# Second layer of a four-layer decoder: gate projections as 16 more columns of the first head's v, and v ahead of q and k

## The chip, the cores and the metric

The kernel runs on one NeuronCore of one Trainium2 chip. The metric is the device time of one execution in microseconds (us). TensorE (PE) multiplies matrices and loads its weights beside that (PEld), VectorE (DVE) and ScalarE (ACT) work on rows of up to 128 partitions, GpSimd (POOL) does small copies and memsets, SyncE (SP) issues the DMAs. Each engine takes its own instructions strictly in the order in which they stand.

## The reference

1040 tokens (16 of a learnt prefix and 1024 of input) of 1024 features pass four layers; each adds a branch to the residual: `h = h + branch(rmsnorm(h, norm_gain[i]))`. Layers 1 and 4 are sliding-window attention, layer 3 is a gated recurrence (HGRN2), and layer 2, which the change touches, is an mLSTM with 8 heads. What matters of it:

```
q, k, v, ig, fg, og, z = split(u @ w_in, (1024, 1024, 2048, 8, 8, 2048, 2048))
q, k = split(silu(causal_conv(concat(q, k), conv_w, conv_b)))     # 4 taps
log_i = ig + bias_i                                               # 8 rows, one for each head
log_f = log_sigmoid(fg + bias_f)
h = chunkwise over blocks of 128 tokens, from q, k, v, log_i, log_f, state C and norm n
h = rmsnorm(sigmoid(og) * h, h_gain) * silu(z);   out = h @ w_out
```

The two gates are thus 16 columns of the big projection, and every head needs them, with running sums and maxima over the tokens, before its first block.

## The kernel before

The activations stand transposed: 8 tiles of 128 features by 1040 tokens, in the residual `x` and, after the norm, split in a high and a low part (`uh`, `ul`), so that a product in full precision is three matmuls (high by high, high by low, low by high) on the fp32r path. Weights come by DMA into `wr` (two buffers) and are split the same way by ACT (`wh`) and DVE (`wl`) into three pairs of buffers; the helper `split` does this everywhere (L187 ACT, L188 DVE). Tokens are worked in three chunks of 400, 384 and 256 (`CHUNKS`), or in 9 blocks (16 tokens, then 8 of 128), of which the chunks hold four, three and two. `proj` (L254) multiplies weights as the stationary side by a chunk of tokens; `proj_v` (L295, L299) takes tokens as the stationary side and 256 columns of v as the moving side, one block at a time, in two halves of the features.

The order of PE is written by hand: every layer hands over a list of steps (cost, function, and a step that fetches its weights ahead), `weave` mixes two lists by their costs, and steps of cost 0 stand for work without matmuls. A layer's `head` runs between the output projection of the layer before and its own `body`; the norm of the second and third chunk (`Norm`: squares, one statistic matmul at L381, eight units at L407 that end in `uh` and `ul`) is placed inside of it. The other engines' order is made by a scheduler from that program, and depends on it.

In the second layer (`layer_b`) the head is, for each chunk, the gates' projection (`gate_rows_proj`, L215: 16 matmuls with one tile that holds the gates' high and low weights), then q and k of head 0. Its result is put together by `gate_evac` (ACT L791, DVE L792). After the last chunk `gate_rows` computes, on 8 partitions by 1040 tokens, log-sigmoid (ACT L797 to L799, DVE L800), a running maximum (L801), running sums by block (L804), their differences (L806, L807) and an exponential (ACT L811). Two results go through DRAM (`rowsd`, L814 and L815) and come back broadcast to 128 partitions (`rb`, `wb`: L882, L883); the other two are transposed on PE by `gate_cols` (L825, L826). `conv_proj` takes q and k out of PSUM (ACT L846), applies the four taps on DVE (L849 and three times L852), and multiplies by the sigmoid (ACT L424 to L426, DVE L427, ACT L428, then DVE L856 for q and L858 for k). The body is v of head 0 with `gate_cols` in its middle, then the `mixer` of each head, woven with the next head's q, k and v. The first step of a mixer's block, `s1`, multiplies k by q and transposes k (L890, L892); its next step, `s2` (L918), needs the decayed weights that DVE and ACT make from `rb` (L903 and on).

Of the kernel before, what the change touches and what calls it, by code (L numbers as in the profile page):

```python
# [36 lines left out]
TAIL_LAG = 2000.0  # L37
PRIO = 40
ROWS, TMPS, RAWS, YS, QS = 9, 5, 2, 3, 6
XS = 14  # L40
GAP, BURST, PAUSE = 200.0, 1300.0, 2500.0
KT_LAG = 500.0
NORM_AT = (4000.0, 0.7), (5000.0, 0.5), (8000.0, 0.5)
# [6 lines left out]
MM = 1.0 / 2.4  # L50
# [18 lines left out]
def flat(groups):  # L69
    return [x for grp in groups for x in grp]  # L70
# [38 lines left out]
def hybrid_kernel(ctx: ExitStack, tc: tile.TileContext, ins, out, layers=(0, 1, 2, 3)):  # L109
    nc = tc.nc  # L110
    v, s, g, pe, sp = nc.vector, nc.scalar, nc.gpsimd, nc.tensor, nc.sync
# [11 lines left out]
    def nm(x):  # L123
        ctr[0] += 1
        return f"{x}{ctr[0]}"
# [11 lines left out]
        return tpool.tile([P, 404], F32, tag="t", name=nm("t"), bufs=TMPS)  # L137

    def small(w):
        return tpool.tile([P, w], F32, tag=f"s{w}", name=nm("s"), bufs=12 if w < 8 else 4)  # L140

    def psum(tag, bufs):
        return ps.tile([P, 512], F32, tag="p", name=nm(tag), bufs=8)
# [1 line left out]
    def psj():  # L145
        return psum("pj", 3)
# [6 lines left out]
    ident = cpool.tile([P, P], F32, name="ident")  # L153
# [32 lines left out]
    def split(src, h, l):  # L186
        s.copy(h, src)  # L187
        v.tensor_tensor(l, src, h.bitcast(F32), op=ALU.subtract)  # L188

    def gate_weights(src):  # L190

        w = wpool.tile([P, 1024], F32R, tag="wh", name=nm("wh"), bufs=3).rearrange("p (k z c) -> p k z c", k=KT, z=2)
        raw = wpool.tile([P, 512], F32, tag="raw", name=nm("wr"), bufs=RAWS)
        sp.dma_start(raw, src)
        raw = raw.rearrange("p (k c) -> p k c", k=KT)
        split(raw, w[:, :, 0], w[:, :, 1])
        return w

    def gate_rows_proj(src, evac):

        st = {}

        def pre():
            st["w"] = gate_weights(src)

        groups = []
        for n, (c0, cn) in enumerate(CHUNKS):
            grp = []
            for part in range(4):
                def fn(n=n, c0=c0, cn=cn, part=part):  # L210
                    if part == 0:
                        st[n] = psj()
                    for k in (2 * part, 2 * part + 1):
                        for i, b in enumerate((uh, ul)):
                            pe.matmul(st[n][:, :cn], st["w"][:, k].rearrange("p z c -> p (z c)"), b[:, k, c0 : c0 + cn],  # L215
                                      start=(k == 0 and i == 0), stop=(k == KT - 1 and i == 1))
                    if part == 3:
                        evac(st[n], n, c0, cn)

                grp.append([4 * cn * MM, fn, pre if (n == 0 and part == 0) else None])  # L220
            groups.append(grp)
        return groups

    def weights(src, kind, inrow=False):
        if inrow:
            h, l = (rrow()[:, :1024] for _ in range(2))
        else:
            h = wpool.tile([P, 1024], F32R, tag="wh", name=nm("wh"), bufs=3)
            l = wpool.tile([P, 1024], F32R, tag="wl", name=nm("wl"), bufs=3)
        for z in (slice(0, 512), slice(512, 1024)):  # L230
            raw = wpool.tile([P, 512], F32, tag="raw", name=nm("wr"), bufs=RAWS)
            sp.dma_start(raw, src[:, z])
            split(raw, h[:, z], l[:, z])
        k = dict(m=8, v=4, o=2)[kind]
        return h.rearrange("p (k c) -> p k c", k=k), l.rearrange("p (k c) -> p k c", k=k)
# [24 lines left out]
            groups.append(grp)  # L260
        return groups

    def put_v(V, acc, b, cn):

        if b == 0:
            s.copy(V[:cn, :256], acc[32 : 32 + cn, :256])
            v.tensor_tensor(V[:cn, :256], V[:cn, :256], acc[:cn, :256], op=ALU.add)
        else:
            s.copy(V[:cn, :256], acc[:cn, :256])

    def proj_v(src0, src1, evac):
        st = {}

        def pre0():
            st[0] = weights(src0, "v")

        def pre1():
            st[1] = weights(src1, "v")

        groups = []  # L280
        for blocks in CHUNK_BLOCKS:
            grp = []
            for b in blocks:
                c0, cn = blk(b)
                for half in range(2):
                    def fn(b=b, c0=c0, cn=cn, half=half):
                        if half == 0:
                            st["a", b] = psj()
                        acc = st["a", b]
                        wh, wl = st[half]  # L290
                        for kk in range(4):
                            k = 4 * half + kk
                            if b == 0:
                                for m in (wh, wl):
                                    pe.matmul(acc[:48, :256], um[:, k, :], m[:, kk, :],  # L295
                                              start=(k == 0 and m is wh), stop=(k == KT - 1 and m is wl))
                            else:
                                for i, (a, m) in enumerate(((uh, wh), (uh, wl), (ul, wh))):
                                    pe.matmul(acc[:cn, :256], a[:, k, c0 : c0 + cn], m[:, kk, :],  # L299
                                              start=(k == 0 and i == 0), stop=(k == KT - 1 and i == 2))  # L300
                        if half == 1:
                            evac(acc, b, c0, cn)

                    grp.append([(8 if b == 0 else 12) * 256 * MM, fn, (pre0, pre1)[half] if b == 0 else None])
            groups.append(grp)
        return groups

# [463 lines left out]
    def layer_b(i, j, fin):  # L771
        win, wout = ins["b_win"][j], ins["b_wout"][j]
        R = {}
# [10 lines left out]
            R["hgain"] = cols[:, 80:96]  # L784
            R["li"], R["lf"] = row(), row()

        def gate_evac(acc, n, c0, cn):
            cs = slice(c0, c0 + cn)
            for key, r, c in (("li", 0, 0), ("lf", 32, 1)):
                z = R[key][:8, cs]  # L790
                s.activation(z, acc[64 + r : 72 + r, :cn], AF.Identity, bias=R["bias"][:, c : c + 1])  # L791
                v.tensor_tensor(z, z, acc[r : r + 8, :cn], op=ALU.add)  # L792

        def gate_rows():
            mix, li, lf = R["mix"], R["li"], R["lf"]
# [66 lines left out]
        def v_evac(h):  # L862
            def f(acc, b, c0, cn):
                hi_ = rpool.tile([P, 258], F32R, tag="v", name=nm("v"), bufs=10)
                lo = R["mix"].tile([P, 256], F32R, tag="vl", name=nm("vl"), bufs=10)
                R["v", h, b] = hi_, lo
                if b == 0:
                    both = tmp()
                    put_v(both, acc, b, cn)
                    acc = both  # L870
                split(acc[:cn, :256], hi_[:cn, :256], lo[:cn])
# [140 lines left out]
        gg = gate_rows_proj(ins["b_wgate"][j], gate_evac)  # L1012
        qg = {h: conv_proj(win[8 * h], h, 1.0, ("q", h)) for h in range(8)}
        kg = {h: conv_proj(win[8 * h + 1], 8 + h, 128 ** -0.5, ("k", h)) for h in range(8)}
        vg = {h: proj_v(win[8 * h + 2], win[8 * h + 3], v_evac(h)) for h in range(8)}
        og = {h: og_proj(h) for h in range(8)}
        zg = {h: [gate_proj(win[8 * h + 6 + c], lambda h=h, c=c: R["h", h, c]) for c in range(2)] for h in range(8)}
        oc = {h: proj_out(wout[2 * h], wout[2 * h + 1], lambda k, h=h: R["h", h, k], CHUNKS,
# [7 lines left out]
                tail = g1[n] + tail  # L1026
            return flat(g0) + tail

        head = [gg[n] + qg[0][n] + kg[0][n] for n in range(3)]
        head[0].insert(0, [0.0, enter, None])  # L1030
        head[2].insert(len(gg[2]), [0.0, gate_rows, None])
        body = flat(vg[0])
        body.insert(len(body) // 2, [18 * 30, gate_cols, None])
        for h in range(8):
            mx = mixer(h)
            mx, rest = mx[:-3], mx[-3:]
# [9 lines left out]
        body = [z for z in body if z[1] is not pause]  # L1046
# [332 lines left out]
    k = 0  # L1379
# [31 lines left out]
def _layout(inp):  # L1411
# [50 lines left out]
    gw = np.zeros((D, 64), np.float32)  # L1462
    gw[:, 0:8] = bw[:, i0 : i0 + 8]
    gw[:, 32:40] = bw[:, f0 : f0 + 8]
    f["b_wgate"] = gw.reshape(KT, P, 64).transpose(1, 0, 2).reshape(1, P, 512)
# [40 lines left out]
```

## Time and profile before

| | us |
|---|---|
| runs | 2610.01, 2610.45, 2611.44 (median 2610.45) |
| profiled execution | 2610.83 |
| its span | 2609.0 |
| PE busy, of the span | 2558.0 |
| DVE busy | 1980.3 |
| ACT busy | 1725.9 |
| second layer's head and first body | about 488 to 553 of the span |

The span is the profiler's, from the first to the last instruction; 1.8 us of the execution's own time lie around it. Busy time of PE counts overlapping matmuls as one stretch, so it says when PE had work, and not how fast it went.

### The profile page before, as it was taken

How to read it: one execution, taken by the hardware profiler on the slowest of the kernel's cores; microseconds unless marked ns; L12 is line 12 of the kernel's file. 1: busy time of each engine (PE TensorE's matmuls, PEld its weight loads, DVE VectorE, ACT ScalarE, POOL GpSimd, SP SyncE). 2: the span in 40 equal slices, each digit the busy share in tenths (PEclk: the TensorE clock that was granted, in tenths of full speed). 3: DMA queues.
4: the chain of work that ended last, by engine and by line, in shares of the span. 5: the costliest groups of instructions: out<-in, count | busy, mean ns of one | idle time of the engine just before them, and what ended most of it. 6: DMA issues, size and time to landing. Idle time of an engine off the chain costs nothing.

```text
span 2609.0 us, 56062 instructions
## 1 busy us (share of the span) xinstructions
PE 2558.0 (98%) x21048; PEld 2459.0 (94%) x21048; DVE 1980.3 (76%) x5487; ACT 1725.9 (66%) x4757; POOL 154.1 (6%) x538
## 2 busy tenths in 40 slices
PE   7999999999999999999999999999999999999999
PEld 6899889899999999999999999999999999999999
DVE  6677777986767676767677788978787978677776
ACT  6777776566464646464646857878585867768872
POOL 1100100000000000000000000201001011000000
PEclk9999999999999999999999999999999999999999
DMA  4111111021111111111110101011110111111112
GB/s 136 56 43 50 46 37 47 17 67 58 41 58 41 58 41 58 41 58 41 55 61 34 57 27 42 30 38 34 34 42 26 42 62 45 54 44 47 53 38 82
DMA packets 74048, 126.81 MB, mean 49 GB/s; under 512 B 11552, under 2 KB 25760, under 8 KB 73776
## 3 DMA queue, kind: packets, MB, share of 16 engines
q1 hardware_dynamic: 73776, 123.23, 14.5%
q8 instruction: 165, 2.70, 0.4%
q14 instruction: 107, 0.88, 0.1%
HBM read 108.34 MB, written 4.26 MB: 43 GB/s over the span
## 4 chain that ended last, share of the span: by engine, by line
PE 81%; DVE 10%; ACT 6%; issue 1%; DMA 1%; POOL 0%; SPq 0%; DVEq 0%; ACTq 0%; POOLq 0%
PE pj L254 39%; PE pj L337 16%; PE pj L299 11%; PE po L682 2%; PE pt L660 1%; PE pm L614 1%; PE pm L615 1%; DVE t L407 1%; PE pa L534 1%; DVE ul L188 1%; PE po L918 1%; PE pj L295 1%; PE pm L890 1%; DVE X L1153 1%; DVE X L1155 1%
## 5 line engine op out<-in xcount | busy, mean ns | idle before, releaser
L254 PE MATMUL pj<-uh,wh 128*128 128x384 f32 (+2 forms) x2592 | 870.9, 336 | 3.7 <-ACT uh L187 3.6
L254 PE MATMUL pj<-ul,wh 128*128 128x384 f32 (+2 forms) x2592 | 835.3, 322 | 2.9 <-DVE ul L188 2.8
L254 PE MATMUL pj<-uh,wl 128*128 128x384 f32 (+2 forms) x2592 | 832.9, 321 | 0.1
L254 PEld LDWEIGHTS pj<-uh,wh 128*128 128x128 f32 x2592 | 491.3, 190 | 24.1 <-issue 12.7
L254 PEld LDWEIGHTS pj<-ul,wh 128*128 128x128 f32 x2592 | 491.2, 190 | 8.7 <-DVE ul L188 5.5
L254 PEld LDWEIGHTS pj<-uh,wl 128*128 128x128 f32 x2592 | 490.9, 189 | 0.5 <-DVE wl L188 0.4
L188 DVE TENSOR_TENSOR wl<-wr,wh 128x512 fp32r<-128x512 f32 x336 | 227.9, 687 | 58.1 <-ACT wh L187 55.4
L340 DVE TENSOR_TENSOR x<-x,pj 128x384 f32<-128x384 f32 (+2 forms) x480 | 235.4, 510 | 43.2 <-PE pj L337 41.3
L187 ACT CAST wh<-wr 128x512 fp32r<-128x512 f32 x337 | 203.3, 616 | 83.0 <-PE pj L337 26.8
L299 PE MATMUL pj<-wh,uh 128*128 128x256 f32 x896 | 258.1, 288 | 0.0
L337 PE MATMUL pj<-yh,wh 128*128 128x384 f32 (+2 forms) x768 | 253.0, 329 | 0.0
L299 PE MATMUL pj<-wh,ul 128*128 128x256 f32 x896 | 252.4, 282 | 0.0
L299 PE MATMUL pj<-wl,uh 128*128 128x256 f32 x896 | 252.3, 282 | 0.0
L337 PE MATMUL pj<-yl,wh 128*128 128x384 f32 (+2 forms) x768 | 247.4, 322 | 3.1 <-DVE yl L188 3.1
L337 PE MATMUL pj<-yh,wl 128*128 128x384 f32 (+2 forms) x768 | 246.8, 321 | 0.0
L299 PEld LDWEIGHTS pj<-wh,uh 128*128 128x128 f32 x896 | 169.3, 189 | 1.1 <-issue 0.3
L187 ACT CAST yh<-r 128x400 fp32r<-128x400 f32 (+2 forms) x144 | 68.6, 477 | 153.2 <-PE pj L337 141.7
L299 PEld LDWEIGHTS pj<-wl,uh 128*128 128x128 f32 x896 | 169.3, 189 | 0.5
L299 PEld LDWEIGHTS pj<-wh,ul 128*128 128x128 f32 x896 | 169.3, 189 | 0.0
L428 ACT ACTIVATE t<-t 128x384 f32<-128x384 f32 (+2 forms) x240 | 117.8, 491 | 76.5 <-DVE t L427 74.8
L427 DVE SCALAR_TENSOR_TENSOR t<-pj,t 128x384 f32<-128x384 f32 (+2 forms) x192 | 98.8, 514 | 78.2 <-ACT t L426 75.3
L337 PEld LDWEIGHTS pj<-yl,wh 128*128 128x128 f32 x768 | 144.9, 189 | 5.0 <-DVE yl L188 4.7
(265 smaller groups left out, 5431.4 us busy)
## 6 DMA issues: line engine op xcount, KB each, us to landing
wr<-in_b_win SPq DMA_DIRECT2D x128, 256.0 KB, 2.6
wr<-in_a_win SPq DMA_DIRECT2D x80, 256.0 KB, 2.7
wr<-in_c_win SPq DMA_DIRECT2D x64, 256.0 KB, 2.7
r<-rowsd SPq DMA_DIRECT2D x16, 520.0 KB, 5.4
wr<-in_a_wout SPq DMA_DIRECT2D x32, 256.0 KB, 2.7
wr<-in_b_wout SPq DMA_DIRECT2D x32, 256.0 KB, 2.6
t<-t SPq DMA_DIRECT2D x96, 48.0 KB, 1.9
wr<-in_c_wout SPq DMA_DIRECT2D x16, 256.0 KB, 2.7
```

Of the source, the lines that this page charges most:

```text
L187: s.copy(h, src)
L188: v.tensor_tensor(l, src, h.bitcast(F32), op=ALU.subtract)
L254: pe.matmul(acc[:, :cn], a[:, k, :], b[:, k, c0 : c0 + cn], start=(k == 0 and i == 0), stop=(k == KT - 1 and i == 2))
L295: pe.matmul(acc[:48, :256], um[:, k, :], m[:, kk, :], start=(k == 0 and m is wh), stop=(k == KT - 1 and m is wl))
L299: pe.matmul(acc[:cn, :256], a[:, k, c0 : c0 + cn], m[:, kk, :], start=(k == 0 and i == 0), stop=(k == KT - 1 and i == 2))
L337: pe.matmul(acc[:, :cn], a[:, k, mc], b, start=(k == 0 and i == 0), stop=(k == 1 and i == 2))
L340: v.tensor_tensor(x[:, m, c0 : c0 + cn], x[:, m, c0 : c0 + cn], acc[:, :cn], op=ALU.add)
L407: v.scalar_tensor_tensor(u, x[:, k, cs], ngain[:, self.i, k : k + 1], self.acc[n], op0=ALU.mult, op1=ALU.mult)
L427: v.scalar_tensor_tensor(a[:, :cn], z, 0.0, a[:, :cn], op0=ALU.min, op1=ALU.subtract)
L428: s.activation(a[:, :cn], a[:, :cn], AF.Exp)
L534: pe.matmul(st[:, 2 * k : 2 * k + 2], sq[:, z : z + P], R["masks"][:, 0:P:64], start=True, stop=True)
L682: pe.matmul(po[64 * hh : 64 * hh + 64, q0 - c0 : q0 - c0 + nq], V[kb][:kn, vc : vc + 64], ws[hh]["Pt"][:kn, u, ki, :nq], start=(ki == 0), ...
```

## The change

The gates' own projection is removed. The first head's `proj_v` gets 16 more columns (`width` 272), whose weights are split into columns 256 to 271 of a wider weight tile. For each block an ACT copy (`gate_part`) takes these columns out of PSUM into a zeroed tile, and after each chunk `gate_turn` transposes that tile on PE, block by block, and ACT writes the gates' rows with their bias. v of head 0 becomes the whole head, `gate_rows` follows its last chunk, and the body begins with q and then k of head 0, with `gate_cols` at three quarters of it. For the room of the wider tiles, the third layer's ring of tiles `X` goes from 14 to 13, and the ring of one-column tiles from 12 to 6.

```diff
-XS = 14
+XS = 13
+WCOLS = 1088
...
-    def weights(src, kind, inrow=False):
+    def weights(src, kind, inrow=False, more=None):
...
+        if more is not None:
+            h, l = (z.rearrange("p (k c) -> p k c", k=4) for z in (h, l))
+            for z in range(2):
+                raw = wpool.tile([P, 512], F32, tag="raw", name=nm("wr"), bufs=RAWS)
+                sp.dma_start(raw, src[:, 512 * z : 512 * z + 512])
+                ks = slice(2 * z, 2 * z + 2)
+                split(raw.rearrange("p (k c) -> p k c", k=2), h[:, ks, :256], l[:, ks, :256])
+            raw = wpool.tile([P, 512], F32, tag="raw", name=nm("wr"), bufs=RAWS)
+            sp.dma_start(raw[:, :64], more)
+            split(raw[:, :64].rearrange("p (k c) -> p k c", k=4), h[:, :, 256:], l[:, :, 256:])
+            return h, l
...
-                                    pe.matmul(acc[:cn, :256], a[:, k, c0 : c0 + cn], m[:, kk, :],
+                                    pe.matmul(acc[:cn, :width], a[:, k, c0 : c0 + cn], m[:, kk, :],
...
-        def gate_evac(acc, n, c0, cn):
-            cs = slice(c0, c0 + cn)
-            for key, r, c in (("li", 0, 0), ("lf", 32, 1)):
-                z = R[key][:8, cs]
-                s.activation(z, acc[64 + r : 72 + r, :cn], AF.Identity, bias=R["bias"][:, c : c + 1])
-                v.tensor_tensor(z, z, acc[r : r + 8, :cn], op=ALU.add)
+        def gate_part(acc, b, cn):
+            n = [b in z for z in CHUNK_BLOCKS].index(True)
+            k = b - CHUNK_BLOCKS[n][0]
+            if k == 0:
+                R["g", n] = tmp()[:, :160].rearrange("p (b c) -> p b c", b=4)
+                g.memset(R["g", n], 0.0)
+            out = R["g", n][:cn, k].rearrange("p (z c) -> p z c", c=8)[:, ::4]
+            s.copy(out, acc[:cn, 256:272].rearrange("p (z c) -> p z c", z=2))
+
+        def gate_turn(n):
+            def fn():
+                c0, cn = CHUNKS[n]
+                pt = psum("pt", 1)
+                for k, b in enumerate(CHUNK_BLOCKS[n]):
+                    q0, nq = blk(b)
+                    pe.transpose(pt[:40, q0 - c0 : q0 - c0 + nq], R["g", n][:nq, k], ident[:nq, :nq])
+                for z, key in enumerate(("li", "lf")):
+                    s.activation(R[key][:8, c0 : c0 + cn], pt[32 * z : 32 * z + 8, :cn], AF.Identity,
+                                 bias=R["bias"][:, z : z + 1])
+
+            return [110.0 * len(CHUNK_BLOCKS[n]), fn, None]
...
-        head = [gg[n] + qg[0][n] + kg[0][n] for n in range(3)]
+        head = [vg[0][n] + [gate_turn(n)] for n in range(3)]
         head[0].insert(0, [0.0, enter, None])
-        head[2].insert(len(gg[2]), [0.0, gate_rows, None])
-        body = flat(vg[0])
-        body.insert(len(body) // 2, [18 * 30, gate_cols, None])
+        head[2].append([0.0, gate_rows, None])
+        body = flat(qg[0]) + flat(kg[0])
+        body.insert(len(body) * 3 // 4, [18 * 30, gate_cols, None])
```

The lines of the changed kernel are some three to twenty smaller: L187 and L188 stay 188 and 189, the conv's L846, L849, L852, L856 and L858 become 841, 844, 847, 851 and 853, `gate_rows` L797 to L811 becomes 792 to 806, L903 becomes 900.

On DVE, the rows that lead up to the product that ends the first chunk of k of head 0 (tile `r_6534` before, `r_6986` in the change; `t` are temporaries, `E` is the first block's decay and `qw` the second's scaled q). Before, it stands among the norm's units of the third chunk:

```order
L856 TENSOR_TENSOR q_6482<-q_6482,t_6489 128x400
L852 SCALAR_TENSOR_TENSOR r_6534<-t_6533,bcols_6391,r_6534 128x400 x3
L407 SCALAR_TENSOR_TENSOR t_6548<-x,ngain,t_6298 128x256
L188 TENSOR_TENSOR ul<-t_6548,uh 128x256
L407 SCALAR_TENSOR_TENSOR t_6552<-x,ngain,t_6298 128x256
L427 SCALAR_TENSOR_TENSOR t_6541<-r_6534,t_6541 128x400
L188 TENSOR_TENSOR ul<-t_6552,uh 128x256
L407 SCALAR_TENSOR_TENSOR t_6561<-x,ngain,t_6298 128x256
L858 SCALAR_TENSOR_TENSOR r_6534<-r_6534,t_6541 128x400
```

In the change, it stands behind the first block's decay (L900), a part of the second chunk of k, and q of the second block (L896):

```order
L847 SCALAR_TENSOR_TENSOR r_6986<-t_6985,bcols_6394,r_6986 128x400
L900 SCALAR_TENSOR_TENSOR E_7112<-r_7105,bcol_7013,caus_6396 16x16
L840 COPY t_7050<-t_6985 128x3
L189 TENSOR_TENSOR wl_7355<-wr_7360,wh_7354 128x512
L844 TENSOR_SCALAR r_6986<-t_7050,bcols_6394 128x384
L847 SCALAR_TENSOR_TENSOR r_6986<-t_7050,bcols_6394,r_6986 128x384
L896 TENSOR_TENSOR qw_7204<-q_6858,r_7106 128x128
L407 SCALAR_TENSOR_TENSOR t_6993<-r_6986,t_6993 128x400
L847 SCALAR_TENSOR_TENSOR r_6986<-t_7050,bcols_6394,r_6986 128x384
L189 TENSOR_TENSOR ql_7207<-qw_7204,qh_7206 128x128
L853 SCALAR_TENSOR_TENSOR r_6986<-r_6986,t_6993 128x400
```

What moved is the conv of head 0: it stood ahead of the gates' chain on DVE, and now stands behind it.

On ACT, the gates' chain and what stands around its exponential. Before, with q and k of head 0 already taken out but for the third chunk:

```order
L797 ACTIVATE r_6712<-r_6398 8x1040
L798 ACTIVATE r_6712<-r_6712 8x1040
L424 ACTIVATE t_6684<-r_6534 128x384
L799 ACTIVATE r_6712<-r_6712,one 8x1040
L425 ACTIVATE t_6684<-t_6684 128x384
L846 COPY t_6768<-pj_6743 128x256
L426 ACTIVATE t_6684<-t_6684,one 128x384
L187 CAST wh_6978<-wr_6980 128x512
L187 CAST wh_6978<-wr_6984 128x512
L428 ACTIVATE t_6684<-t_6684 128x384
L811 ACTIVATE r_6397<-r_6713 8x16
L811 ACTIVATE r_6397<-r_6713,r_6712 8x128 x8
```

In the change:

```order
L792 ACTIVATE r_6801<-r_6401 8x1040
L793 ACTIVATE r_6801<-r_6801 8x1040
L188 CAST wh_6930<-wr_6932 128x512
L794 ACTIVATE r_6801<-r_6801,one 8x1040
L841 COPY t_6857<-pj_6832 128x400
L188 CAST wh_6930<-wr_6936 128x512
L188 CAST wh_7137<-wr_7139 128x512
L806 ACTIVATE r_6400<-r_6802 8x16
L806 ACTIVATE r_6400<-r_6802,r_6801 8x128 x8
L404 ACTIVATE t_6865<-q_6858 128x400
L841 COPY t_6897<-pj_6872 128x384
```

Of q's three chunks (L841, from PSUM) the first is now taken out in the middle of the chain, and the second only behind its exponential.

## Rows read from the trace of the kernel before

**Rows 1.** The page's first part, engine PE: busy us, share, instructions.

```profile
PE 2558.0 (98%) x21048; PEld 2459.0 (94%) x21048; DVE 1980.3 (76%) x5487; ACT 1725.9 (66%) x4757; POOL 154.1 (6%) x538
```

**Rows 2.** Stretches: length, busy us of PE, PEld, DVE, ACT, POOL; PE clock, DMA.

```profile
510.00:520.00 10.00, 8.14 (x37) 6.38 (x36) 8.90 (x20) 5.25 (x12) 0.00 (x0) 0.85 0.01 2
520.00:530.00 10.00, 10.00 (x72) 10.00 (x72) 7.58 (x17) 8.99 (x16) 0.00 (x0) 0.81 0.31 105
```

**Rows 3.** Timeline of PE, second layer's head and body: start us, duration, instruction.

```profile
488.10 0.64 PE L215 MATMUL pj<-uh,wh 128*128 128x400 f32 x1
491.30 0.35 PE L254 MATMUL pj<-uh,wh 128*128 128x400 f32 x1
...
503.94 0.44 PE L215 MATMUL pj<-ul,wh 128*128 128x384 f32 x1 [0.57 <-DVE ul L188]
504.22 0.34 PE L254 MATMUL pj<-uh,wh 128*128 128x384 f32 x1
...
512.67 0.28 PE L215 MATMUL pj<-uh,wh 128*128 128x256 f32 x1
...
519.26 0.41 PE L254 MATMUL pj<-uh,wh 128*128 128x256 f32 x1
...
523.74 0.33 PE L254 MATMUL pj<-uh,wh 128*128 128x256 f32 x1
...
538.86 0.17 PE L825 MATMUL pt<-ident,r 8*16 8x8 f32 x1
...
539.99 0.38 PE L299 MATMUL pj<-wh,uh 128*128 128x256 f32 x1
...
552.95 0.22 PE L890 MATMUL pm<-q,r 128*16 128x16 f32 x2
```

**Rows 4.** Timeline of DVE: the norm's last unit and the gates' chain.

```profile
518.41 0.42 DVE L188 TENSOR_TENSOR ul<-t,uh 128x256 fp32r<-128x256 f32 x1
...
529.63 1.23 DVE L800 SCALAR_TENSOR_TENSOR r<-r,r 8x1040 f32<-8x1040 f32 x1 [1.56 <-ACT r L799]
531.58 2.30 DVE L801 TENSOR_TENSOR_SCAN r<-r,r 8x1040 f32<-8x1040 f32 x1
534.26 2.70 DVE L804 TENSOR_TENSOR_SCAN r<-ones,r 8x16 f32<-8x16 f32 x9
538.82 1.22 DVE L807 TENSOR_TENSOR r<-r,r 8x1040 f32<-8x1040 f32 x1
```

**Rows 5.** Timeline of ACT: the gates' chain.

```profile
525.83 1.06 ACT L797 ACTIVATE r<-r 8x1040 f32<-8x1040 f32 x1
...
540.19 2.44 ACT L811 ACTIVATE r<-r,r 8x128 f32<-8x128 f32 x8
```

**Rows 6.** DVE from 500 to 550 by line and shape: busy us, mean ns, idle before.

```profile
L188 DVE TENSOR_TENSOR wl<-wr,wh 128x512 fp32r<-128x512 f32 x6 | 3.8, 677 | 0.1
L852 DVE SCALAR_TENSOR_TENSOR q<-t,bcols,q 128x400 f32<-128x400 f32 x3 | 1.9, 634 | 0.1
L852 DVE SCALAR_TENSOR_TENSOR q<-t,bcols,q 128x256 f32<-128x256 f32 x3 | 1.4, 460 | 0.0
L427 DVE SCALAR_TENSOR_TENSOR t<-r,t 128x400 f32<-128x400 f32 x1 | 0.6, 575 | 0.2 <-ACT t L426 0.2
L849 DVE TENSOR_SCALAR q<-t,bcols 128x384 f32<-128x384 f32 x1 | 0.5, 481 | 0.1
```

**Rows 7.** Timeline of PE, first matmuls of the kernel, after its first waits.

```profile
14.90 0.70 PE L254 MATMUL pj<-uh,wh 128*128 128x400 f32 x1 [3.02 <-ACT uh L187]
...
18.71 0.34 PE L254 MATMUL pj<-uh,wh 128*128 128x400 f32 x1
```

**Rows 8.** DMA issues from 535 to 555: KB each, median us to landing.

```profile
r<-rowsd SPq DMA_DIRECT2D x2, 520.0 KB, 4.7
```

**Rows 9.** Waits of PE, then of DVE, in the third layer (1580 to 2130).

```profile
PE pm L1178 <- DVE X L1155: 2.5, 1, 2.5
...
DVE X L1152 <- PE pt L1228: 24.3, 10, 6.3
```

More of the change, by code (lines that the diff above doesn't have):

```diff
@@ L139, in small @@
     def small(w):
-        return tpool.tile([P, w], F32, tag=f"s{w}", name=nm("s"), bufs=12 if w < 8 else 4)
+        return tpool.tile([P, w], F32, tag=f"s{w}", name=nm("s"), bufs={1: 6, 2: 12}.get(w, 4))
     def psum(tag, bufs):
@@ L188, in split @@
         v.tensor_tensor(l, src, h.bitcast(F32), op=ALU.subtract)
[L190 to L222, printed above, removed]
-    def weights(src, kind, inrow=False):
+    def weights(src, kind, inrow=False, more=None):
         if inrow:
@@ L227, in weights @@
         else:
-            h = wpool.tile([P, 1024], F32R, tag="wh", name=nm("wh"), bufs=3)
-            l = wpool.tile([P, 1024], F32R, tag="wl", name=nm("wl"), bufs=3)
+            h = wpool.tile([P, WCOLS], F32R, tag="wh", name=nm("wh"), bufs=3)
+            l = wpool.tile([P, WCOLS], F32R, tag="wl", name=nm("wl"), bufs=3)
+        if more is not None:
[9 more added lines that the diff above has]
+            return h, l
+        h, l = h[:, :1024], l[:, :1024]
         for z in (slice(0, 512), slice(512, 1024)):
@@ L261, in proj, with put_v, proj_v @@
         return groups
-    def put_v(V, acc, b, cn):
+    def put_v(V, acc, b, cn, w=256):
         if b == 0:
-            s.copy(V[:cn, :256], acc[32 : 32 + cn, :256])
-            v.tensor_tensor(V[:cn, :256], V[:cn, :256], acc[:cn, :256], op=ALU.add)
-        else:
-            s.copy(V[:cn, :256], acc[:cn, :256])
-    def proj_v(src0, src1, evac):
+            s.copy(V[:cn, :w], acc[32 : 32 + cn, :w])
+            v.tensor_tensor(V[:cn, :w], V[:cn, :w], acc[:cn, :w], op=ALU.add)
+        else:
+            s.copy(V[:cn, :w], acc[:cn, :w])
+    def proj_v(src0, src1, evac, more=(None, None)):
         st = {}
+        width = 256 if more[0] is None else 272
         def pre0():
-            st[0] = weights(src0, "v")
+            st[0] = weights(src0, "v", more=more[0])
         def pre1():
-            st[1] = weights(src1, "v")
+            st[1] = weights(src1, "v", more=more[1])
         groups = []
@@ L294, in fn @@
                                 for m in (wh, wl):
-                                    pe.matmul(acc[:48, :256], um[:, k, :], m[:, kk, :],
+                                    pe.matmul(acc[:48, :width], um[:, k, :], m[:, kk, :],
                                               start=(k == 0 and m is wh), stop=(k == KT - 1 and m is wl))
@@ L302, in fn @@
                             evac(acc, b, c0, cn)
-                    grp.append([(8 if b == 0 else 12) * 256 * MM, fn, (pre0, pre1)[half] if b == 0 else None])
+                    grp.append([(8 if b == 0 else 12) * width * MM, fn, (pre0, pre1)[half] if b == 0 else None])
             groups.append(grp)
@@ L868, in f @@
                     both = tmp()
-                    put_v(both, acc, b, cn)
+                    put_v(both, acc, b, cn, 256 if h else 272)
                     acc = both
+                if h == 0:
+                    gate_part(acc, b, cn)
                 split(acc[:cn, :256], hi_[:cn, :256], lo[:cn])
@@ L1010, in og_proj @@
             return g0, g1, [stat(n, *CHUNKS[n]) for n in range(3)]
-        gg = gate_rows_proj(ins["b_wgate"][j], gate_evac)
+        wgate = ins["b_wgate"][j]
         qg = {h: conv_proj(win[8 * h], h, 1.0, ("q", h)) for h in range(8)}
         kg = {h: conv_proj(win[8 * h + 1], 8 + h, 128 ** -0.5, ("k", h)) for h in range(8)}
-        vg = {h: proj_v(win[8 * h + 2], win[8 * h + 3], v_evac(h)) for h in range(8)}
+        vg = {h: proj_v(win[8 * h + 2], win[8 * h + 3], v_evac(h),
+                        (None, None) if h else (wgate[:, :64], wgate[:, 64:])) for h in range(8)}
         og = {h: og_proj(h) for h in range(8)}
@@ L1461, in _layout @@
     f["b_wout"] = _opieces(np.asarray(inp["b_w_out"])[0], np.arange(2048))[None]
[L1462 to L1465, printed above, removed]
+    gw = np.concatenate([bw[:, i0 : i0 + 8], bw[:, f0 : f0 + 8]], axis=1)
+    f["b_wgate"] = gw.reshape(KT, P, 16).transpose(1, 0, 2).reshape(1, P, 128)
     cw = np.concatenate([np.asarray(inp["b_conv_w"])[0], np.asarray(inp["b_conv_b"])[0][None]])
```

## The prediction

> **What bounds the kernel now.** I read the page first, then stretches of 10 us around the second layer's head, then each engine's timeline there, then the waits of the third layer. The page [rows 1] shows PE busy for 98% of the span: the kernel is bound by PE's own list, and a change can gain by taking matmuls out or by closing one of the few places where PE waits. The stretches [rows 2] show one of these: from 510 to 520 PE is busy for 8.14 of 10 us, and the granted clock of 0.85 and 0.81 says that part of both stretches ran at half speed (1.2 in place of 2.4 GHz). The timeline [rows 3] places it: the gates' matmuls of the third chunk begin at 512.67 and end only at 519.26, because the norm's last units come late on DVE (the last `ul` is written at 518.41 to 518.83 [rows 4]), and the 21 matmuls from 519.26 to 523.74 start 0.213 us apart, where 108 of the same shape from 539.99 to 552.95 start 0.120 apart. From 523.74 to the mixer's first step at 552.95 PE is never kept waiting. DVE is the engine to watch: busy for 8.90 and 7.58 of these 10 us [rows 2], with the gates' chain of 8-row passes of 1.2 to 2.7 us [rows 4], since a pass over 8 partitions by 1040 tokens costs by its columns.
>
> I use the span's clock of before; the changed head also begins at 488.10.
>
> **What the change takes out and adds on PE.** Out go the gates' three stretches: 488.10 to 491.30 is 3.2; the second is 16 matmuls at 0.176 (48 from 504.22 to 512.67) and the wait of 0.57, so 3.4; the third is 6.6 with its waits; and 21 x 0.093 = 2.0 for the half clock that follows [rows 3]. Sum 15.2, if the norm's third chunk is then in time. It should be: DVE loses from its list ahead of 518.8 the conv of q and k's first chunk and of a part of q's second, some 13 instructions of 0.48 to 0.63 [rows 6] and four additions of `gate_evac` of about 0.5, together some 8 us, so the last unit comes near 511; PE wants it at 513.4 (below).
>
> In come 16 columns on 208 matmuls: 128 columns more cost 0.176 - 0.120 = 0.056, so 16 cost 0.007 each, 1.5 in all. In come nine transposes, at 0.063 each by the 18 of `gate_cols` (538.86 to 539.99 [rows 3]), 0.6. They stand right behind the matmuls of their chunk, so PE waits three times for a round trip: the last matmul's way through (0.41 is the longest record of this shape), an ACT copy of 16 columns (no such row; under the 0.31 of one of the eight pieces of L811 [rows 5]) and two hand-overs; from 0.4 to 1.5 each, I take 0.8, so 2.4. PE alone would thus reach the mixer's first step at 552.95 - 15.2 + 1.5 + 0.6 + 2.4 = 542.2, a gain of 10.7.
>
> A page speaks against these three waits: the Trainium skill, "TensorE: Matmul & The Clock Gate", section "A second HAM failure mode: psum-queue depth-cycling", holds that short idles between groups of matmuls, when frequent, make the clock swing between its two levels. The trace does not bear it out for one such gap: after the wait of 0.57 at 503.94 the next 48 matmuls ran at full speed [rows 3]. By the rows the three waits cost 2.4; by the page each could add a half-clock stretch of 2, which is a rival below.
>
> **What it moves.** v needs only copies, so the conv of head 0 now comes behind the gates' chain on ACT and DVE, as the two orders show, and the mixer's first step needs the first chunk of k. I follow that chain. v ends at 488.1 + 208 x 0.127 + two round trips with their transposes (2.0) = 516.5, its sums are out at about 517. ACT copies the columns, splits v, writes the two gate rows after the transposes: 1.5 for four passes of 0.3 to 0.5. Then two of three passes of 1.06 [rows 5], a weight split of 0.6, the third pass: 522.3. DVE then does L800's pass (1.2), a tap of q (0.48), the scans of 2.3 and 2.7, a tap (0.63), a difference (1.2, from which `gate_cols` on PE is fed, at about 530.5; PE comes there at 535.5, so no wait), a tap, and the other difference (1.2) [rows 4, 6]: 10.3, less some overlap, so 532.3. ACT's exponential (2.44 and a short piece) ends at 534.9 [rows 5], and only behind it stand the sigmoid's first pass and the copy of q's second chunk out of PSUM, 0.5 each: 535.9.
>
> From there DVE's list up to the product that ends k's first chunk holds 34 instructions: 4 first taps (0.48), 11 further taps (three of 0.63, five of about 0.61, three of 0.46), four L427 and four products (0.42 to 0.58), three weight splits (0.68), and eight short ones (decay, q of the second block, copies; no rows of their own here, together 1.4): 1.9 + 6.3 + 4.1 + 2.0 + 1.4 = 15.7 [rows 6]. End to end that is 551.6. Below, instructions that don't depend on each other overlap by up to 0.08, which gives 549; above, six hand-overs to ACT and back at half a us each give 554.6. I keep 551.6, since the two pull against each other. The broadcast `rb`, which the decay ahead of it needs, is issued behind a weight load at about 539 and lands 4.7 later [rows 8], at 544, some 3 us before DVE comes to it.
>
> So PE, ready at 542.2, waits until 551.6 for k: 9.4 us, and the 10.7 are taken back. After such a wait it starts at half clock: after 3.02 of waiting the first matmuls of the kernel were slow from 14.90 to 18.71 [rows 7], and 4.5 us were slow above; half of 3.8 to 4.5 is lost, so 1.9 more. Seen from PE the mixer's first step is at 551.6 + 0.1 + 1.9 = 553.6 in place of 552.95: +0.65. From there the order on PE is the same to the end. DVE still has k's other two chunks to finish, some 4 us, under the 4.4 of the next head's q that PE does before the first block's `s2`; I count nothing for it.
>
> **The smaller ring.** With 13 tiles `X` DVE can run one tile less ahead of PE in the third layer. PE waited for `X` there once, 2.5 us; DVE waited ten times for PE to free one [rows 9], which is where a smaller ring bites. One tile's work is three DVE passes and one of ACT, 1.2 at most (four of 0.3); where DVE is well ahead this costs nothing. Between 0 and seven such regions (8.4), nearer to the one wait seen: I take 1.0. The ring of one-column tiles holds one for a block at a time; 6 do. Nothing.
>
> **Sum:** 2610.83 (this execution's own time, 0.4 above the median of the runs) + 0.65 + 1.0 = 2612.5. 0.2%, about what a measurement of this kernel can tell from no change, is 5.2 us.
>
> **Rivals.**
> 1. The vector side keeps up and PE collects what it was freed of. For it: PE is the bound everywhere else, and in before nothing waited from 523.74 on. Against it: 15.7 us of DVE's list behind the exponential. Without any wait 2610.8 - 10.7 = 2600; it decides from a wait under 3.6 us, which asks DVE's list to be 5.8 shorter than I sum. 0.15.
> 2. The ring of 13 sets PE back in the third layer (slower): if seven of the forty regions start 1.2 later, and one wait drops the clock, 2611.5 + 8.4 + 2 = 2622; it decides from 4.5 us, four such regions. Against it: PE's only wait for `X` of before. 0.13.
> 3. The page's short idles: the clock falls at the first two turns, each costs 2.0 ahead of the gates' chain, which moves as a whole: 2612.5 + 4 = 2616.5, and with a chunk of norm late more. 0.05.
> 4. `rb` lands late, because it now stands behind two weight loads on SP's queue that wait for their buffers; the decay stands ahead of k's product in DVE's list, so everything waits. It must be over 7 us later than I put it: 2618. 0.05.
>
> **How the numbers follow.** The forecast (the wait for k eats the gain) has 0.62, and alone reaches from 549 to 554.6 for that wait's end and 0 to 3 for the ring: 2609 to 2617. Leaving out the far half of rival 1 and the far part of 2 gives 2605.5 to 2618.5. Faster is rival 1, 0.15; slower are 2 to 4, 0.23; the rest, 0.62, is no change.
>
> **What would show it.** No waits for `uh` and `ul` of the third chunk and no half clock near 515; three gaps of about 0.8 at the transposes; PE's first long wait, 9 us, at the mixer's first k-by-q, ended by DVE's product of k, and slow matmuls behind it; that step at 551.7 on the span's clock. Wrong, if that wait is under 5 us or over 14, if PE waits at `gate_cols`, or if the second layer comes out even and the third layer's waits for `X` make the difference.

## The result, and the profile after

| | before | changed |
|---|---|---|
| median, us | 2609.77 (22 runs) | 2613.86 (22 runs) |
| profiled execution, us | 2610.83 | 2615.78 |
| its span, us | 2609.0 | 2614.0 |

The ratio is 1.0014, 95% interval 1.0008 to 1.0020: the change costs 2 to 5 us, 4.1 by the medians. (One run of the changed kernel took 6589 us at a mean granted clock of 0.47; it is left out of the ratio, and without it the median is 2613.80.) The forecast was 2612.5 and "no change that can be told", the range 2605.5 to 2618.5.

The page's first line of the changed kernel, which answers to [rows 1], shows PE with 5.5 us less work in a span that is 5 us longer:

```profile
PE 2552.5 (98%) x21009; PEld 2453.5 (94%) x21009; DVE 1977.0 (76%) x5482; ACT 1727.4 (66%) x4767; POOL 152.6 (6%) x541
```

The stretches say where it went. The columns are those of [rows 2], for the changed kernel:

```profile
510.00:520.00 10.00, 9.80 (x76) 9.23 (x75) 4.84 (x13) 5.39 (x15) 0.43 (x7) 1.00 0.14 45
520.00:530.00 10.00, 10.00 (x65) 10.00 (x64) 6.87 (x13) 4.74 (x7) 0.00 (x0) 1.00 0.19 64
540.00:550.00 10.00, 3.15 (x26) 2.95 (x25) 8.70 (x24) 6.91 (x19) 0.00 (x0) 0.91 0.44 159
550.00:560.00 10.00, 7.38 (x28) 7.05 (x29) 7.23 (x21) 5.51 (x14) 0.00 (x0) 0.58 0.08 29
```

The hole of [rows 2] at 510 to 520 is gone, with its clock of 0.85 and 0.81. A new one stands at 540 to 552, with 0.58 behind it. The waits of PE from 480 to 620 (us in total, times, longest) name three places:

```profile
PE pm L887 <- issue: 9.5, 1, 9.5
PE pt L782 <- ACT t L774: 1.6, 2, 1.5
PE pj L317 <- DVE yl L189: 0.7, 1, 0.7
```

The last of them stands before the head, in both kernels. In the timeline of PE, the head begins at 488.59 (488.10 in [rows 3]: this execution came out of the first layer 0.49 later, which is taken off wherever the two are compared below). The end of k, the first step of the mixer and the matmuls behind it:

```profile
488.59 0.58 PE L275 MATMUL pj<-wh,um 128*48 128x272 f32 x1
...
502.51 0.29 PE L782 MATMUL pt<-ident,t 128*40 128x128 f32 x1 [1.49 <-ACT t L774]
...
518.31 0.27 PE L782 MATMUL pt<-ident,t 128*40 128x128 f32 x1
...
542.87 0.28 PE L233 MATMUL pj<-uh,wl 128*128 128x256 f32 x1
552.62 0.21 PE L887 MATMUL pm<-q,r 128*16 128x16 f32 x2 [9.47 <-issue]
552.76 0.38 PE L889 MATMUL pm<-ident,r 128*16 128x128 f32 x1
552.80 0.68 PE L233 MATMUL pj<-uh,wh 128*128 128x400 f32 x1
553.28 0.54 PE L233 MATMUL pj<-ul,wh 128*128 128x400 f32 x1
...
558.28 0.42 PE L233 MATMUL pj<-ul,wh 128*128 128x400 f32 x1
558.54 0.34 PE L233 MATMUL pj<-uh,wl 128*128 128x400 f32 x1
```

The profile puts the wait of 9.47 to "issue", that is, to nothing it can see. DVE's timeline shows what ended just before 552.62 (the start of the mixer's first step): the product that ends k's first chunk, L853, from 551.95 to 552.52.

```profile
532.44 1.22 DVE L802 TENSOR_TENSOR r<-r,r 8x1040 f32<-8x1040 f32 x1
...
548.42 0.22 DVE L900 SCALAR_TENSOR_TENSOR E<-r,bcol,caus 16x16 f32<-16x16 f32 x1
...
551.95 0.57 DVE L853 SCALAR_TENSOR_TENSOR r<-r,t 128x400 f32<-128x400 f32 x1
552.43 0.61 DVE L847 SCALAR_TENSOR_TENSOR r<-t,bcols,r 128x384 f32<-128x384 f32 x1
```

On ACT the gates' exponential stands ahead of q's sigmoid and of the copy of its second chunk, as the order said:

```profile
533.82 2.44 ACT L806 ACTIVATE r<-r,r 8x128 f32<-8x128 f32 x8
536.16 0.52 ACT L404 ACTIVATE t<-q 128x400 f32<-128x400 f32 x1
536.59 0.45 ACT L841 COPY t<-pj 128x384 f32<-128x384 f32 x1
```

**Where the 5 us of the profiled executions come from.** From the head's first matmul to the mixer's first step: 64.85 before, 64.03 in the changed kernel, so 0.8 gained. From 552.80 to 558.28 sixteen matmuls of 400 columns run, 0.333 apart but for the first, where they run 0.18 apart at full clock: 2.6 lost. A little later DVE's backlog delays one `s2` by 0.5. By then the second layer is 2.2 behind. The third layer adds 3.7 up to its last products of `X`; 0.5 was there before the head. The third layer's part is in part the ring and in part a lower clock near its start, as the experiments show. Then 1.6 comes back in the fourth layer, all of it between 2190 and 2205, and not by anything that the change does there: PE is busy for the same 13.36 of 15 us in both kernels, but the granted clock fell in the execution of before and not in that of the changed kernel (before first):

```profile
2190.00:2205.00 15.00, 13.36 (x87) 11.94 (x86) 13.05 (x30) 12.23 (x30) 1.70 (x3) 0.89 0.19 54
```

```profile
2190.00:2205.00 15.00, 13.36 (x83) 11.99 (x82) 14.28 (x33) 12.84 (x31) 1.70 (x3) 1.00 0.19 51
```

### The profile page after: what moved, and what is told of

The parts are those of the page before. It is cut to its first block, busy times and chain, and to the rows that moved or that the text cites. A ratio compares the mean times of both kernels' runs of the same rounds, so it can differ in the third digit from the quotient of the medians.

```text
span 2614.0 us, 55987 instructions
## 1 busy us (share of the span) xinstructions
PE 2552.5 (98%) x21009; PEld 2453.5 (94%) x21009; DVE 1977.0 (76%) x5482; ACT 1727.4 (66%) x4767; POOL 152.6 (6%) x541
## 4 chain that ended last, share of the span: by engine, by line
PE 81%; DVE 10%; ACT 6%; issue 2%; DMA 1%; POOL 0%; SPq 0%; DVEq 0%; ACTq 0%; POOLq 0%
PE pj L233 39%; PE pj L317 16%; PE pj L279 10%; PE po L662 2%; PE pt L640 1%; PE pm L594 1%; PE pm L595 1%; PE pa L514 1%; DVE t L387 1%; PE po L915 1%; DVE ul L189 1%; DVE wl L189 1%; PE pm L887 1%; DVE x L320 1%; PE po L917 1%
## 5 line engine op out<-in xcount | busy, mean ns | idle before, releaser
L189 DVE TENSOR_TENSOR wl<-wr,wh 128x512 fp32r<-128x512 f32 (+1 forms) x338 | 228.4, 684 | 62.6 <-ACT wh L188 60.1
L188 ACT CAST wh<-wr 128x512 fp32r<-128x512 f32 (+1 forms) x338 | 203.2, 614 | 91.7 <-PE pj L317 30.9
L279 PE MATMUL pj<-wh,uh 128*128 128x256 f32 (+1 forms) x896 | 259.0, 289 | 0.0
L279 PE MATMUL pj<-wh,ul 128*128 128x256 f32 (+1 forms) x896 | 253.3, 283 | 0.0
L279 PE MATMUL pj<-wl,uh 128*128 128x256 f32 (+1 forms) x896 | 252.7, 282 | 0.0
L188 ACT CAST yh<-r 128x400 fp32r<-128x400 f32 (+2 forms) x144 | 68.6, 477 | 152.7 <-PE pj L317 141.5
```

Of the source, the lines that this page charges most:

```text
L279: pe.matmul(acc[:cn, :width], a[:, k, c0 : c0 + cn], m[:, kk, :], start=(k == 0 and i == 0), stop=(k == KT - 1 and i == 2))
```

## The experiments

Each was timed in five rounds beside the kernel before, on the same chip (e9, e10 and e11 on another chip than the rest); the differences below are to the median of those runs. With 11 runs each (10 for e10), one of less than some 2.3 us is not told apart from nothing; profiles resolve more, stretch by stretch.

### The ring alone: e1, e2, e10

```diff
e1, the kernel before:
-XS = 14
+XS = 13
e2, the changed kernel:
-XS = 13
+XS = 14
e10, the changed kernel:
-XS = 13
+XS = 12
```

> The kernel before with one edit, the third layer's ring of X at 13 tiles in place of 14. Theory A (the ring's step of the prediction, a few regions start later): 0 to 3 us slower than before, so 2610 to 2613. Theory B (the ring makes most of the 4 us by which the change is slower): 3 to 5 us slower, and the PE waits in the third layer grow by as much. Theory C (the ring is free and the 4 us come from the second layer alone): within 1 us of before.

> The changed kernel with the ring of X back at 14 tiles, nothing else. Theory A: 0 to 3 us faster than the changed kernel, 2611 to 2614. Theory B: 3 to 5 faster, 2609 to 2611, and in the third layer PE no longer falls back by 3.4 us against before. Theory C: no difference. In all of them the second layer keeps its wait of 9.5 us at the mixer's first step.

> The changed kernel with a ring of 12 tiles X, one less again. Theory A (each tile that the ring lacks costs 2 us, in the third layer between 1700 and 2100): another 2 to 4 us there and 2615 to 2618, with PE's idle time in that stretch up by 1.4 or more. Theory B (the ring has no part in it, and what the profiles with 13 share is chance): no change against the changed kernel.

Measured: e1 2611.7, 1.9 above before (ratio 1.0006, 0.9997 to 1.0015); e2 2613.5, 3.7 above (1.0012, 1.0003 to 1.0021); e10 2617.9, 6.4 above (1.0023, 1.0013 to 1.0032), while the changed kernel itself is 4.1 above. So the three single tiles cost 1.9, 0.4 and 2.3 by the medians. The timeline of PE at the third layer's last group of 15 products of `X` is sharper. The rows are those of before, e1, e2, the changed kernel and e10, one each:

```profile
2103.08 0.50 PE L1168 MATMUL pm<-X 128*32 128x64 f32 x15
```

```profile
2105.68 0.50 PE L1168 MATMUL pm<-X 128*32 128x64 f32 x15
```

```profile
2105.41 0.50 PE L1166 MATMUL pm<-X 128*32 128x64 f32 x15
```

```profile
2109.56 0.50 PE L1166 MATMUL pm<-X 128*32 128x64 f32 x15
```

```profile
2110.50 0.50 PE L1166 MATMUL pm<-X 128*32 128x64 f32 x15
```

The heads of the five begin at 488.10, 487.94, 486.41, 488.59 and 487.87, so the stretch from there is 1614.98, 1617.74, 1619.00, 1620.97 and 1622.63 long. A tile less costs 2.8 (before to e1), 2.0 (e2 to the changed kernel) and 1.7 (the changed kernel to e10). The stretch from 1700 to 2100 speaks against chance: PE's busy time goes with the ring, before and e2 (14), then e1 and the changed kernel (13), in this order:

```profile
1700.00:2100.00 400.00, 394.63 (x5157) 378.35 (x5157) 336.57 (x1115) 294.95 (x843) 39.74 (x97) 1.00 0.11 35
```

```profile
1700.00:2100.00 400.00, 394.72 (x5264) 378.25 (x5263) 336.08 (x1117) 294.47 (x845) 38.64 (x97) 1.00 0.11 35
```

```profile
1700.00:2100.00 400.00, 393.11 (x5181) 376.51 (x5170) 335.97 (x1114) 293.59 (x839) 37.92 (x97) 1.00 0.11 35
```

```profile
1700.00:2100.00 400.00, 393.80 (x5259) 377.22 (x5259) 334.11 (x1104) 292.07 (x835) 38.11 (x97) 1.00 0.11 36
```

The later profiles agree: with 14 tiles e5, e7, e8, e9 and e11 show 394.6 to 395.0 there, with 13 tiles e3, e4 and e6 show 393.1 to 393.5. So theory A holds by the profiles: the ring is worth about 2 us a tile at the third layer's end. The times of e1 and e2 alone do not tell A from C. What comes back in the fourth layer is the clock again: it also fell near 2196 in e2 (0.89 from 2190 to 2205), and not in e1 and e10 (1.00), so some 1.6 of the lead of before and e2 goes there, behind the same waits (last section).

Two rows fit less well. With 12 the stretch from 1700 shows 393.79, no less than with 13, against theory A; what the third tile costs stands earlier, in a wait of PE for `X` of 1.7 between 1605 and 1645 that the changed kernel does not have. And e3 and e7 (below), which differ by the ring alone, are only 0.4 apart from the head to this place; from 1620 to 1640 e7, with 14, has a granted clock of 0.91 where e3 has 1.00.

Not all of the third layer's 3.7 is the ring: e2, with 14, takes 1.8 more from 584 to this place than before does, with a granted clock of 0.91 and 0.91 from 1620 to 1640 and 1640 to 1660 where before has 1.00 and 0.92. The changed kernel and e10 have 0.91 and 0.91 there too, and e1 has 1.00 and 0.92. It is no part of what the change computes: in e2 the ring of 14 stands beside the wider weight tiles. Whether it is chance or follows from when the third layer begins is open.

### q and k chunk by chunk: e3

```diff
-        body = flat(qg[0]) + flat(kg[0])
+        body = flat(qg[0][n] + kg[0][n] for n in range(3))
```

> The changed kernel with the body of the second layer's head in another order: q and k of head 0 chunk by chunk (q, k of the first chunk, then of the second, then of the third) in place of all q, then all k. The product that ends the first chunk of k stands 20 instructions behind the gates' last difference on DVE in place of 37. Theory A (PE waits for k because of its place in DVE's list): the wait of 9.5 us becomes about 5, its end then set by the broadcast that E needs (lands at about 544, and E stands ahead of the product), and the time 4 to 5 us less, about 2609.5. Theory B (the wait is for something else at that step, such as q or the broadcast itself): wait within 1 us of 9.5, time unchanged.

Measured: 2607.4, 2.4 below before (0.9993, 0.9984 to 1.0001) and 6.4 below the changed kernel. The waits of PE from 480 to 620, and DVE around the product:

```profile
PE po L915 <- ACT wd L188: 2.5, 3, 1.3
PE pm L887 <- issue: 1.9, 1, 1.9
```

```profile
539.69 0.22 DVE L900 SCALAR_TENSOR_TENSOR E<-r,bcol,caus 16x16 f32<-16x16 f32 x1 [0.26 <-DMA r<-rowsd]
...
543.16 0.56 DVE L853 SCALAR_TENSOR_TENSOR r<-r,t 128x400 f32<-128x400 f32 x1
543.64 0.16 DVE L840 COPY t<-t 128x3 f32<-128x3 f32 x1
```

The place in DVE's list decides, theory A: the product ends at 543.72 and PE begins at 543.82. The wait fell further than expected, to 1.9, since the broadcast landed before 539.7 and not at 544 (its load is issued 48.0 us after the head's start, against 51.8 in the changed kernel). The clock stays at 1.00 here. The first step comes 7.7 us earlier, counted from the head, and the half clock's 2.6 are saved too, 10.3 in all; of these 6.4 are left in the time. A new wait, of the mixer for `wd`, takes 2.5 of the rest.

### Work put ahead of the wait: e4

```diff
-                body += weave(mx, flat(qg[h + 1]) + flat(kg[h + 1]) + flat(vg[h + 1]))
+                fill = flat(qg[h + 1]) + flat(kg[h + 1]) + flat(vg[h + 1])
+                lead = 8 if h == 0 else 0
+                body += mx[:1] + fill[:lead] + weave(mx[1:], fill[lead:])
```

> The changed kernel with the first eight steps of the next head's q (its first two chunks, 8.6 us of PE) put ahead of the mixer's first step of head 0. Theory A (the wait for k is a pure wait behind DVE, and the half clock follows from it): the wait shrinks to about 1 us, no half clock behind it, and the time is 8.5 + 2.9 = 11.4 us less than the changed kernel, about 2602.5. Theory B (the vector side as a whole is the limit in this stretch, so the work put ahead is only missed later): new waits inside the mixer of head 0, and a gain under 4 us.

Measured: 2608.3, 1.5 below before (0.9992, 0.9983 to 1.0001), 5.6 below the changed kernel: between the two theories. The wait went down to 0.8, and this time the profile names what it is for. The waits, then the stretches:

```profile
PE po L915 <- ACT wd L188: 4.2, 4, 1.5
...
PE pm L887 <- DVE r L853: 0.8, 1, 0.8
...
PE po L917 <- DVE wl L189: 0.5, 1, 0.5
```

```profile
550.00:560.00 10.00, 8.41 (x59) 7.50 (x58) 9.22 (x26) 7.22 (x21) 0.14 (x2) 1.00 0.07 27
560.00:570.00 10.00, 9.27 (x58) 8.54 (x56) 9.89 (x31) 7.00 (x20) 0.13 (x2) 1.00 0.16 55
570.00:580.00 10.00, 7.39 (x60) 7.07 (x60) 9.69 (x34) 7.35 (x22) 0.13 (x2) 1.00 0.00 0
```

PE idles for 4.9 of these 30 us while DVE is busy for 28.8. Of the 11.4 us that were to be had, half went back as waits for the decayed weights, which DVE and ACT make.

### The order alone: e5, and with e3's body: e9

```diff
e5, the kernel before:
-        head = [gg[n] + qg[0][n] + kg[0][n] for n in range(3)]
+        head = [gg[n] + vg[0][n] for n in range(3)]
...
-        body = flat(vg[0])
-        body.insert(len(body) // 2, [18 * 30, gate_cols, None])
+        body = flat(qg[0]) + flat(kg[0])
+        body.insert(len(body) * 3 // 4, [18 * 30, gate_cols, None])
e9, in e5:
-        body = flat(qg[0]) + flat(kg[0])
+        body = flat(qg[0][n] + kg[0][n] for n in range(3))
```

> The kernel before with the change's order alone: the gates keep their own projection (48 matmuls), but v of head 0 follows it in the head, and q, then k of head 0 make the body. Worked out: the gates' third chunk is out 3.5 us earlier than in the changed kernel, since no block of v stands ahead of it, so their chain and the k behind it come 3.5 earlier, near 548.5; PE, with 7.9 us of gates' matmuls and no late norm, is ready at 545.2. Theory A (when the chain starts decides when k comes): a wait of about 3 at the mixer's first step and a time of 2606 to 2609, faster than the changed kernel although PE has more matmuls. Theory B (the matmuls that are taken out are what counts): slower than the changed kernel by the 5 us of PE work it keeps, over 2616.

> The kernel before with the order of e5 (the gates' own projection, then v, in the head) and the body of e3 (q and k of head 0 chunk by chunk), ring of 14: it is the kernel of e7 with the gates' 48 matmuls kept. PE is ready at the mixer's first step 57.2 us after the head's start (as in e5), and k, as in e7, about 56 after it. Theory A (the vector side sets this stretch, and the matmuls that the change removes are worth little): the first step 57.2 to 58 after the head's start against 56.5 in e7, and a time within 1.5 us of e7. Theory B (with k no longer late, the removed matmuls count in full): 4 to 5 us slower than e7.

Measured: e5 2609.2, 1.5 below before (0.9994, 0.9985 to 1.0003); e9 2608.4, 3.1 below (0.9992, 0.9983 to 1.0001), where e7, the same with the matmuls taken out, is 3.7 below. PE's long wait in e5:

```profile
PE pm L890 <- DVE r L858: 6.2, 1, 6.2
```

PE was ready 57.2 us after the head's start, as worked out, and waited until 63.4; the changed kernel begins that step at 64.0, with some 5 us of matmuls fewer. Theory B of both falls: the matmuls that the change removes are worth nothing behind e5's order, where e2, the change with the same ring, is 3.7 above before and e5 1.5 below; and they are worth 0.6 between e9 and e7, which is inside the noise. Theory A's time for e5 was too good by up to 3: the gates' last chunk is there earlier, but its four passes over 8 rows and the casts between them take that up, and ACT's first pass of the chain begins at 516.65, 30.6 after the head's start, against 31.5 in the changed kernel. In e9 the first step comes after 57.1 with no wait at all, and the waits stand behind it (2.5 for `wd`, 1.2 for `wl`). Two of them, 1.47 and 1.22 us long and ending at 551.46 and 553.08, were followed by a half clock in this execution, with the matmuls of 384 columns 0.32 apart up to 560.92:

```profile
550.00:560.00 10.00, 7.32 (x27) 6.27 (x28) 9.09 (x31) 7.36 (x22) 0.14 (x2) 0.72 0.17 52
```

### The gates' chain made shorter: e6

```diff
-            v.tensor_tensor_scan(m[:8, :], lf[:8, :], li[:8, :], 0.0, ALU.add, ALU.max)
-            for b in range(NB):
-                c0, cn = blk(b)
-                v.tensor_tensor_scan(a[:8, c0 : c0 + cn], ones[:8, :cn], lf[:8, c0 : c0 + cn], 0.0,
-                                     ALU.mult, ALU.add)
-            v.tensor_tensor(bs[:8, :], li[:8, :], a[:8, :], op=ALU.subtract)
-            v.tensor_tensor(a[:8, :], a[:8, :], m[:8, :], op=ALU.subtract)
+            v.tensor_tensor(bs[:8, :], li[:8, :], lf[:8, :], op=ALU.subtract)
+            v.tensor_tensor(a[:8, :], lf[:8, :], m[:8, :], op=ALU.subtract)
```

> The changed kernel without the running maximum and the running sums of the gates on DVE (L796 and the nine of L799, 5.0 us of DVE in the profile); the two differences read what stands there in their place, so the gates' values are others. Theory A (k waits behind the gates' chain): the product of k comes 4 to 5 us earlier, the wait of 9.5 becomes 4.5 to 5.5, and the time is 4 to 5 less, 2609 to 2610 (up to 2.6 less again if the clock no longer falls). Theory B (k is late because of the conv's own work on DVE and ACT): wait within 1.5 us of 9.5.

Measured: 2607.9, 2.8 below before (0.9991, 0.9982 to 1.0000), 6.9 below the changed kernel when each is taken against its own before. PE's wait:

```profile
PE pm L882 <- issue: 4.5, 1, 4.5
```

Five us of DVE's work ahead of the conv are gone, and the wait is 5.0 shorter, one for one: theory A, k waits behind the gates' chain. The first step comes 59.2 us after the head's start, 4.9 earlier than in the changed kernel; the clock still falls behind it. That the median gained 2 more than these 4.9 is within the interval.

### Adding up: e7, e8, e11

```diff
e7, in e3:
-XS = 13
+XS = 14
e8, in e7:
-        head = [vg[0][n] + [gate_turn(n)] for n in range(3)]
+        head = [list(vg[0][n]) for n in range(3)]
+        head[1].insert(2, gate_turn(0))
+        head[2].insert(2, gate_turn(1))
+        head[2].append(gate_turn(2))
e11, in e7:
-                body += weave(mx, flat(qg[h + 1]) + flat(kg[h + 1]) + flat(vg[h + 1]))
+                qk, vv = flat(qg[h + 1]) + flat(kg[h + 1]), flat(vg[h + 1])
+                body += weave(mx, qk + vv if h else qk[:16] + weave(qk[16:], vv))
```

> The changed kernel with q and k of head 0 chunk by chunk, and the ring of X back at 14. If the two steps add up (6.4 for the order by the run alone, 2 for the ring by the two profiles): 2605 to 2606, and 3.5 to 4.5 us faster than before. If the ring is nothing: 2607.4 as without it.

> The kernel with q and k chunk by chunk and 14 tiles X, and the transposes of a chunk's gates one block of v later (those of the last chunk stay where they are). Theory A (after the reordering the start of the gates' chain, the end of v, still sets everything): PE's wait of 1.5 at the first transposes goes, v ends 1.5 earlier, and all of it is kept: 1 to 1.5 less than without this edit, about 2604. Theory B (DVE, full from 550 to 580, is the limit by now): v ends 1.5 earlier and the waits in the mixer of head 0 grow by as much; within 0.5 us.

> The kernel of e7, and under the mixer of head 0 the next head's last two chunks of k are woven with its v (in place of all q, all k, then v), so that the convs of the next head, which load DVE, are spread over more of the mixer. Theory A (PE's waits between 560 and 580 come from DVE, which is busy for 9.8 of 10 us there): the 2.4 us of waits in that stretch go, and the time is 1 to 2.5 us less than e7. Theory B (they come from the mixer's own chain of steps, whatever DVE has beside it): unchanged.

Measured: e7 2607.0, 3.7 below before (0.9990, 0.9981 to 0.9999); e8 2606.5, 4.2 below (0.9987, 0.9978 to 0.9995); e11 2607.4 on another chip, 4.1 below (0.9986, 0.9978 to 0.9995). All three beat both kernels, by little, and can't be told from each other. In e8 the wait of 1.5 at the first transposes is gone, but PE now comes too early for the norm's second chunk:

```profile
504.03 0.40 PE L279 MATMUL pj<-wh,uh 128*128 128x272 f32 x1 [0.68 <-ACT uh L188]
...
504.81 0.39 PE L279 MATMUL pj<-wh,ul 128*128 128x272 f32 x1 [0.27 <-DVE ul L189]
```

The first step stands 56.3 after the head's start, against 56.5 in e7: what the edit gave was taken by the next thing in line, the norm, which neither theory had. In e11 the waits in the mixer are 3.0 (for `wl` and `wd`) against 2.4 in e7: spreading the next head's k did not take them away. Whether they come from DVE's load or from the mixer's own chain is left open; e4's stretches speak for the load, e11 doesn't.

## Why the prediction was right, step by step

Times are on the clock of [rows 3], that is, 0.49 less than the changed kernel's own.

- **The gates' own projection out, the norm in time.** Right. The last two `ul` of the third chunk begin at 511.0, forecast 511; no wait and no half clock near 515.
- **PE alone ready at 542.2.** It was at 542.7. The transposes' waits were 1.6 in place of 2.4, but nearly all at the first turn, where ACT's copy stood behind casts of the norm that wait for DVE; v with its round trips took 1.3 more than summed.
- **The rule of the page on short idles** (the Trainium skill, "TensorE: Matmul & The Clock Gate", section "A second HAM failure mode: psum-queue depth-cycling"). At the transposes the trace does not agree: after the wait of 1.49 the granted clock stays 1.00, so rival 3 did not happen, and in e4 five waits of up to 1.5 behind the first step leave it at 1.00 (the three stretches above). Elsewhere the traces are in line with it: short waits were followed by a half clock in e9 (0.72) and near 2196 in before (0.89), though not in every execution, as the last section shows.
- **k behind the gates' chain.** Right, and shown: by e6, where 5.0 of DVE's work less is 5.0 of waiting less, and by e3, where only the place in the list changes. The exponential ended at 535.8 (forecast 534.9), k's product at 552.0 (forecast 551.6), the wait was 9.5 (forecast 9.4). `rb` was there before E asked for it at 548.4, so rival 4 did not happen.
- **The half clock behind the wait.** Right, but mis-sized (and [rows 7], from which it was taken in part, are the kernel's first matmuls and no clear case of a wait): 1.9 forecast from half of 3.8 to 4.5, 2.6 measured, since 5.5 us ran slow.
- **Nothing behind it.** Not quite: 0.5 at an `s2`, from the backlog on DVE. Together the second layer gives +2.2, forecast +0.65.
- **The smaller ring, +1.0.** Right in kind, under-sized: about 2 in the third layer for a tile, and at the end, by the medians, 1.9 (e1) and 0.4 (e2) for the tile that the change takes, 1.2 as a mean. That is below the 4.5 at which rival 2 would have decided.
- **Rival 1**, that the vector side keeps up, is refuted by the wait; e5 and e9 show more, that the removed matmuls had no worth that can be told from nothing in either order tried.

2.2 and 1.2 make 3.4 of the measured 4.1; the remainder is inside the interval, and the lower clock near the third layer's start, which the forecast had no term for, may be part of it. The forecast's 1.65 was thus short by the sizes of its terms (the half clock, the ring) and by the `s2` that it put at nothing, and not by the mechanism. That 2612.5 lies only 1.4 below the measured median, where the increase was 2.4 short, is luck: the sum starts from a profiled execution 1.1 above the median of before.

## What to carry to other kernels

Where PE is busy for 98%, taking matmuls out still gains nothing if the vector engines' list, at the next place where PE needs them, is as long as before: follow that list to the product PE waits for, before pricing the matmuls. What stands first in it is worth more than how much PE has to do: one line that puts k's first chunk behind q's took 6 us out, where 5 us of matmuls had taken none. And a ring of tiles that is cut to make room has a price in another layer, which shows in that layer's stretch more clearly than in the time, once the granted clock of the stretches compared has been checked.

## What was not expected of the hardware

The same wait of 1.86 us before the mixer's first step left the granted clock at 1.00 in e3 and e7, and brought it to 0.83 over these 10 us in e8 and e11, though e7 and e11 have the same program up to there. The rows are the stretch of e3 and of e11:

```profile
540.00:550.00 10.00, 8.14 (x53) 7.38 (x52) 9.37 (x26) 7.94 (x24) 0.00 (x0) 1.00 0.12 41
```

```profile
540.00:550.00 10.00, 8.14 (x49) 7.90 (x49) 9.35 (x28) 7.35 (x20) 0.00 (x0) 0.83 0.20 71
```

The first step's matmuls after it are 0.333 apart until 548.67 in e8, and 0.18 apart from the start in e3. So a wait of this length may or may not cost the clock, some 1.6 us, from one execution to the next.

Shorter waits do the same. In the fourth layer, near 2195 in before, PE waits four times, 0.31, 0.64, 0.31 and 0.38 us, and the changed kernel waits there for the same four times. Before and e2 came out of them at a clock of 0.89 over the 15 us, the changed kernel, e1 and e10 at 1.00 (rows in the section on the result), which is the 1.6 us that came back there. And the waits of up to 1.5 in the mixer of head 0 dropped the clock in e9 and not in e3 and e4. Two profiles can thus differ by 1.6 us at one place though PE waits there alike in both, so the granted clock of a stretch is to be read before its length is.
